# A feed-forward stage emitted as one chain of slots, with weight factors made three slots ahead

## The chip, the core and the metric

The kernel runs on one core of a Trainium2 chip. The metric is device time in microseconds (us) for one launch of the whole program, as the median over runs; lower is better.

## What is computed

The reference is one step of a hybrid decoder layer with 1024 prompt tokens and 8 sample tokens, model width 1024. A feed-forward stage with half weight stands before and after the mixers:

```python
def swiglu(x, w_gate, w_up, w_down):
    return (jax.nn.silu(x @ w_gate) * (x @ w_up)) @ w_down
...
D_FF = ((8 * D_MODEL // 3 + 127) // 128) * 128
...
    x = x + (0.5 * swiglu(rms_norm(x, g_ffn1), w1_gate, w1_up, w1_down)).astype(x.dtype)
...
    x = x + (mixed @ w_out).astype(x.dtype)
    x = x + memory_attend(rms_norm(x, g_cross), mem_k, mem_v, w_cq, w_co).astype(x.dtype)
    x = x + (0.5 * swiglu(rms_norm(x, g_ffn2), w2_gate, w2_up, w2_down)).astype(x.dtype)
```

`D_FF` is 2816, which is 22 blocks of 128 hidden columns. Between the two feed-forward stages lie the attention, state-space and cross-attention stages; the change doesn't touch them. All data is float32.

## The kernel before

The function `ffn` is called twice, here FFN1 and FFN2. Activations lie with the model width on the partitions and the tokens along the row, in three groups: P0 and P1 of 388 tokens and a rest R of 256. A float32 product is made of three matmuls on a high and a low part of each operand (`three`, L332: high by high, high by low, low by high), so every weight tile and every activation is split: ScalarE casts the high part, then VectorE or GpSimd subtracts it for the low part (`split`, L319 and L320, for weights; `put`, L264 and L265, for activations).

P0 and P1 together are computed by a Strassen-Winograd scheme: a two-by-two block product takes seven products in place of eight. The names are those of the scheme: A11, A12, A21, A22 are blocks of weights, S1 to S4 sums of them (`add_up`, L366, on VectorE); B11, B21, B22 and T1 to T4 are the matching activations. The rest R is computed directly from A11, A12, A21 and A22.

`gate_up(m)` makes one block of 128 hidden columns. Its eight weight factors are used in the order of the table `ORDER`. Each product leaves its result in one of three PSUM banks, from which `evac` takes it at once: L399 is the ScalarE copy of bank 1 into bank 2 that seeds it, L402 and L408 copy partial results, L405 and L415 are the silu, L411, L414, L416 and L428 are VectorE work, and L393 (ScalarE `tv`) with L394 (VectorE) forms the rest's hidden values, whose high part is `hRh`.

After two blocks, `down(m)` multiplies the pair of hidden blocks with two rows of the down weights, in two column halves, c = 0 and 1, each for two units (u = 0 and 1). There are two sets of PSUM banks; a unit takes one set and each `gate_up` takes one. L499 seeds bank 2 from bank 1 on ScalarE; L501 to L518 are VectorE's adds from a bank onto the residual `x` in SBUF. A set can be used again only when such an add or copy has read it. The eleventh pair is "plain": it goes through `down_last`, which the change leaves alone (the `pd` products). So there are 20 full pairs in the program, each 396 matmuls at L332: 84 with 388 columns and 48 with 256 in each of its three blocks.

Weights come from HBM by DMAs that SyncE issues, 512 KB each, into two raw buffers (tag `wr`); split factors lie in four buffers (tag `w`):

```python
    def raw_(src):
        t = wp.tile([128, 1040], F32, name="fraw", tag="wr", bufs=2)[:, :1024]
        st["load"] = nc.sync.dma_start(t if len(src.shape) == 2 else t.rearrange("p (k c) -> p k c", c=src.shape[2]), src).ins
        return t
```

The load into a raw buffer is issued when the last engine that reads its old content is done. What sets the order of work on each engine before is the framework's scheduler, which simulates a timeline over the whole program and reorders the source; each engine then takes its instructions strictly in that order, and waits where one isn't ready.

Of the kernel before, what the change touches and what calls it, by code (L numbers as in the profile page):

```python
# [10 lines left out]
F32 = mybir.dt.float32  # L11
# [65 lines left out]
def tile_step(ctx, tc, a, o):  # L77
# [257 lines left out]
    ORDER = (("A11", 0, "B11", True), ("S2", 1, "T2", False), ("A12", 0, "B21", False), ("S3", 1, "T3", False),  # L335
             ("S1", 2, "T1", True), ("S4", 2, "B22", False), ("A22", 1, "T4", False), ("A21", None, None, False))
# [4 lines left out]
    def ffn(x, F, wg, wu, wd, fin, turn, mid=None):  # L341
# [27 lines left out]
        def gate_up(m):  # L369
            q = m % 2  # L370
            g_, u_ = raw_(cols_of(wg, m * 128)), raw_(cols_of(wu, m * 128))
            t = {"A11": g_[:, :512], "A12": g_[:, 512:], "A21": u_[:, :512], "A22": u_[:, 512:]}
            bk, rb = bank_set()
            b1, b2, b3 = bk
            sums = sums_of(m)
            e = {}

            def mat(name):
                if name == "S2":
                    add_up("S1", t, sums[:, :512])  # L380
                if name in SUMS and name not in t:
                    add_up(name, t, sums[:, :512] if name == "S3" else sums[:, 512:1024])
                return split(two(512), t[name])

            def rest(name, w):
                i = name in ("A21", "A22")
                first, last = name in ("A11", "A22"), name in ("A12", "A21")
                for j in range(4):
                    three(rb[:, int(i)], w, j, F["R"][j + (4 if name in ("A12", "A22") else 0)], first and j == 0, last and j == 3)

            def rest_end():
                gr, hr = u1_(NR), u1_(NR)
                nc.scalar.activation(gr, rb[:, 0], AF.Silu)  # L393
                nc.vector.scalar_tensor_tensor(hr, rb[:, 1], 0.5, gr, op0=OP.mult, op1=OP.mult)  # L394
                put(Hd["R"][q], hr, nc.vector)

            def evac(name):
                if name == "A11":
                    nc.scalar.copy(b2, b1)  # L399
                elif name == "S2":  # L400
                    e["U2"] = acc_(PA)
                    nc.scalar.copy(e["U2"], b2)  # L402
                elif name == "A12":
                    e["g0"] = g1_(PA)
                    nc.scalar.activation(e["g0"], b1, AF.Silu)  # L405
                elif name == "S3":
                    e["U3"] = acc_(PA)
                    nc.scalar.copy(e["U3"], b2)  # L408
                elif name == "S1":
                    e["u1"] = sq_(PA)  # L410
                    nc.vector.tensor_add(e["u1"], b3, e["U3"])  # L411
                elif name == "S4":
                    g1, u1 = g1_(PA), e["u1"]
                    nc.vector.tensor_add(g1, b3, e["U2"])  # L414
                    nc.scalar.activation(g1, g1, AF.Silu)  # L415
                    nc.vector.scalar_tensor_tensor(u1, u1, 0.5, g1, op0=OP.mult, op1=OP.mult)  # L416
                    if Hd["plain"]:
                        put(Hd["B22" if q else "B12"], u1, nc.vector)
                    elif q:
                        b12, t1 = Hd["b"]  # L420
                        nc.vector.tensor_sub(t1, u1, t1)
                        put(Hd["T2"], t1, nc.vector)
                        put(Hd["B22"], u1, nc.gpsimd)
                        nc.vector.tensor_sub(b12, u1, b12)
                        put(Hd["T3"], b12, nc.gpsimd)
                elif name == "A22":
                    u0, u1 = sq_(PA), e["u1"]
                    nc.vector.scalar_tensor_tensor(u0, b2, 0.5, e["g0"], op0=OP.mult, op1=OP.mult)  # L428
                    put(Hd["B21" if q else "B11"], u0, nc.vector)
                    if Hd["plain"]:  # L430
                        pass
                    elif q:
                        t2 = Hd["b"][1]
                        nc.vector.tensor_sub(u0, u0, t2)
                        put(Hd["T4"], u0, nc.gpsimd)
                    else:
                        nc.vector.tensor_sub(u0, u1, u0)
                        put(Hd["T1"], u0, nc.gpsimd)
                        Hd["b"] = (u1, u0)

            late = m == 0
            early = {}
            for name, b, f, first in ORDER:
                if late and name == "A21":
                    continue
                if name == "S3":
                    early["S1"] = mat("S1")
                w = early.pop(name, None) or mat(name)
                if f:
                    for j in range(4):  # L450
# [1330 lines left out]
```

## Time and profile before

| what | value |
|---|---|
| median of 3 runs | 2690.99 us (2689.28 to 2700.45) |
| profiled execution, its own time | 2690.33 us |
| its span in the profile | 2688.5 us |
| mean granted TensorE clock | 0.971 of full |
| TensorE busy | 2513.5 us, 93% |
| VectorE, ScalarE, GpSimd busy | 67%, 44%, 34% |
| FFN1, first to last matmul at L332 | 105.7 to 800.7 us |
| FFN2, first to last matmul at L332 | 1949.0 to 2640.4 us |

The span is what the profiler saw between the first and last instruction; the program's own time has 1.8 us more around it. The granted clock is the share of full speed that the chip let TensorE run at.

### The profile page before, as it was taken

How to read it: one execution, taken by the hardware profiler on the slowest of the kernel's cores; microseconds unless marked ns; L12 is line 12 of the kernel's file. 1: busy time of each engine (PE TensorE's matmuls, PEld its weight loads, DVE VectorE, ACT ScalarE, POOL GpSimd, SP SyncE). 2: the span in 40 equal slices, each digit the busy share in tenths (PEclk: the TensorE clock that was granted, in tenths of full speed). 3: DMA queues.
4: the chain of work that ended last, by engine and by line, in shares of the span. 5: the costliest groups of instructions: out<-in, count | busy, mean ns of one | idle time of the engine just before them, and what ended most of it. 6: DMA issues, size and time to landing. Idle time of an engine off the chain costs nothing. (4 is left out here: it accounts for less than half of the span.)

```text
span 2688.5 us, 42038 instructions
## 1 busy us (share of the span) xinstructions
PE 2513.5 (93%) x15999; PEld 2387.5 (89%) x15999; DVE 1809.4 (67%) x3660; ACT 1170.4 (44%) x2415; POOL 907.7 (34%) x675
## 2 busy tenths in 40 slices
PE   6899999999999999988996899989699999999998
PEld 6899999999998999987585899978689999999997
DVE  7566666666656657879578947564776666666665
ACT  5433333333334446554576523232344333333345
POOL 5433333333334111125265644102443333333333
PEclk9999999999999999999997999999899999999999
DMA  5412111211113222335756314573011111111112
GB/s 170 135 49 63 58 56 57 64 57 56 57 50 110 76 63 69 102 116 188 250 168 200 116 54 135 180 228 103 24 40 55 48 48 48 55 48 49 55 48 79
DMA packets 270930, 243.66 MB, mean 91 GB/s; under 512 B 16624, under 2 KB 241064, under 8 KB 270720
## 3 DMA queue, kind: packets, MB, share of 16 engines
q1 hardware_dynamic: 269056, 240.88, 29.1%
q8 instruction: 126, 2.06, 0.3%
q14 instruction: 76, 0.62, 0.1%
q10 hardware_dynamic: 1672, 0.09, 0.0%
HBM read 200.02 MB, written 45.75 MB: 91 GB/s over the span
## 5 line engine op out<-in xcount | busy, mean ns | idle before, releaser
L235 POOL TENSOR_TENSOR wl<-wr,wh 128x1024 fp32r<-128x1024 f32 (+4 forms) x79 | 168.2, 2130 | 562.7 <-ACT wh L231 495.7
L320 POOL TENSOR_TENSOR fw<-fraw,fw 128x512 fp32r<-128x512 f32 x131 | 174.6, 1333 | 469.1 <-ACT fw L319 407.9
L320 POOL TENSOR_TENSOR fw<-fs,fw 128x512 fp32r<-128x512 f32 x128 | 172.5, 1348 | 398.4 <-ACT fw L319 367.2
L319 ACT CAST fw<-fs 128x512 fp32r<-128x512 f32 x256 | 158.3, 618 | 270.1 <-PE fb L332 160.0
L319 ACT CAST fw<-fraw 128x512 fp32r<-128x512 f32 x262 | 162.1, 619 | 192.3 <-PE fb L332 189.0
L366 DVE TENSOR_TENSOR fs<-fraw 128x512 f32<-128x512 f32 (+1 forms) x168 | 100.4, 598 | 138.7 <-DMA fraw<-in_w_up_dram 65.9
L320 DVE TENSOR_TENSOR fw<-fraw,fw 128x512 fp32r<-128x512 f32 x131 | 103.3, 788 | 112.8 <-ACT fw L319 112.7
L320 DVE TENSOR_TENSOR fw<-fs,fw 128x512 fp32r<-128x512 f32 x128 | 95.5, 746 | 97.7 <-ACT fw L319 97.7
L332 PE MATMUL fb<-hRh,fw 128*128 128x256 f32 x640 | 137.3, 280 | 0.5
L231 ACT CAST wh<-wr 128x1024 fp32r<-128x1024 f32 (+1 forms) x80 | 76.7, 959 | 111.5 <-PE pwa L245 43.5
L332 PEld LDWEIGHTS fb<-hRh,fw 128*128 128x128 f32 x640 | 109.2, 188 | 3.7 <-DVE x L516 3.7
L245 PE MATMUL pxbc<-xh,wh 128*128 128x344 f32 x288 | 94.7, 329 | 1.6 <-DVE xr L882 1.6
L245 PE MATMUL pqkv<-xh,wh 128*128 128x344 f32 x288 | 93.9, 326 | 0.4 <-DVE x L546 0.3
L245 PE MATMUL pxbc<-xh,wl 128*128 128x344 f32 x288 | 93.8, 326 | 0.0
L245 PE MATMUL pxbc<-xl,wh 128*128 128x344 f32 x288 | 93.2, 324 | 0.0
L245 PE MATMUL pqkv<-xh,wl 128*128 128x344 f32 x288 | 93.0, 323 | 0.0
L245 PE MATMUL pqkv<-xl,wh 128*128 128x344 f32 x288 | 92.8, 322 | 0.0
L332 PE MATMUL fb<-hRl,fw 128*128 128x256 f32 x320 | 87.7, 278 | 0.0
L411 DVE TENSOR_TENSOR tu<-fb,ts 128x388 f32<-128x388 f32 x44 | 24.7, 562 | 90.3 <-ACT ts L408 90.3
L1052 ACT ACTIVATE pr<-pr,nm 128x128 f32<-128x128 f32 (+3 forms) x64 | 49.9, 779 | 56.9 <-DVE nm L1050 51.7
L1050 DVE CUSTOM_DVE_ANT_0 pr<-ps,U 128x128 f32<-128x128 f32 (+3 forms) x64 | 48.0, 751 | 33.5 <-PE ptr L1065 19.5
L332 PE MATMUL fb<-T2h,fw 128*128 128x388 f32 x160 | 54.6, 362 | 17.0 <-ACT fb L499 17.0
(798 smaller groups left out, 9425.1 us busy)
## 6 DMA issues: line engine op xcount, KB each, us to landing
fraw<-in_w_gate_dram SPq DMA_DIRECT2D x44, 512.0 KB
fraw<-in_w_up_dram SPq DMA_DIRECT2D x44, 512.0 KB
fraw<-in_w_down_dram SPq DMA_DIRECT2D x44, 512.0 KB
wr<-in_w_in_dram SPq DMA_DIRECT2D x32, 512.0 KB
x_scr<-x SPq DMA_DIRECT2D x16, 516.0 KB
x<-x_scr SPq DMA_DIRECT2D x16, 516.0 KB
bc<-acs_scr SPq DMA_DIRECT2D x16, 512.0 KB
ckv<-in_cache_mem_k_dram SPq DMA_DIRECT2D x16, 512.0 KB
```

Of the source, the lines that this page charges most:

```text
L231: nc.scalar.copy(hi[:, :w], raw[:, :w])
L235: e.tensor_sub(lo[:, q], raw[:, q], hi[:, q].bitcast(F32))
L245: nc.tensor.matmul(ps, w, v, start=i == 0, stop=i == last)
L319: nc.scalar.copy(hi, src)
L320: (nc.vector if st["turn"] else nc.gpsimd).tensor_sub(lo, src, hi.bitcast(F32))
L332: nc.tensor.matmul(ps, l[:, js], m, start=bool(start and not i), stop=bool(stop and i == 2), skip_group_check=True)
L366: nc.vector.tensor_tensor(dst, t[p], t[q], op=op)
L411: nc.vector.tensor_add(e["u1"], b3, e["U3"])
L1050: nc.vector.tensor_tensor_reduce(pr[:, :w], ps[:, :w], U[:, 896 - b * 128:1024], -1.0, 3e38, OP.add, OP.min, nm)
L1052: nc.scalar.activation(pr[:, :w], pr[:, :w], AF.Exp, scale=-1.0, bias=nm, accum_out=sm)
```

## The change

`gate_up` and `down` no longer emit instructions. They return lists of slots; a slot is a maker of weight factors, the product that uses them, and evacuation events. A new function `run` strings the slots of all pairs into one chain. For slot i it emits first the weight factors of slot i+3 (the load, the sums, the cast, the subtraction), then the matmuls of slot i, then one pending event of each earlier slot, then the first event of slot i. On TensorE, VectorE, ScalarE and GpSimd the order of execution within `ffn` is that of this emission; SyncE's queue is still ordered by the scheduler.

Besides that: S1 is now the second product of `gate_up` and comes before S2; its result is copied aside on ScalarE, and S3's result is added from its bank in place of being copied. In `down` the four weight factors of a half are used in the order A11 with A21 (`first`), S1 with S2 (`sums12`), S3 with S4 (`sums34`), A12 with A22 (`final`). The low parts of all `down` factors go to GpSimd (before, VectorE and GpSimd took turns). The add of a `down` unit onto P0 after A12 becomes `moved`: a ScalarE copy out of the bank and a GpSimd add, in place of one VectorE add (80 of each in the program). The matmuls are the same in number and size. VectorE has 160 instruction rows fewer, GpSimd 160 more.

```diff
-    def split(hl, src, like=lambda t: t):
+    def split(hl, src, like=lambda t: t, eng=None):
         hi, lo = like(hl[0]), like(hl[1])
-        st["turn"] = not st.get("turn")
+        if not eng:
+            st["turn"] = not st.get("turn")
+            eng = nc.vector if st["turn"] else nc.gpsimd
         nc.scalar.copy(hi, src)
-        (nc.vector if st["turn"] else nc.gpsimd).tensor_sub(lo, src, hi.bitcast(F32))
+        eng.tensor_sub(lo, src, hi.bitcast(F32))
...
+            for name, b, f, first, evs in (
+                    ("A11", 0, "B11", True, (seed,)), ("S1", 2, "T1", True, (kept("s1", 2),)), ("S2", 1, "T2", False, (kept("U2", 1),)),
+                    ("A12", 0, "B21", False, (silu,)), ("S3", 1, "T3", False, (up1,)), ("S4", 2, "B22", False, (gate1, hid1, hid1b)),
+                    ("A22", 1, "T4", False, (hid0, hid0b)), ("A21", None, None, False, (rest_end, rest_end2))):
...
+                out.append((lambda name=name: mat(name), product(name, b, f, first, late), evs))
...
+                    if names[0] in SUMS:
+                        i = 0 if names[0] == "S1" else 2
+                        for j, nm in enumerate(names):
+                            add_up(nm, t, t["sums"][:, (i + j) * 256:(i + j + 1) * 256])
+                        hl = split(two(512), t["sums"][:, i * 256:(i + 2) * 256], eng=nc.gpsimd)
...
+                        hl = split(two(512), t["wa" if names[0] == "A11" else "wb"], twice, eng=nc.gpsimd)
...
+                def add(x_, b):
+                    nc.vector.tensor_add(x_, x_, b)
+                def moved(x_, b):
+                    t_ = acc_(PA)
+                    nc.scalar.copy(t_, b)
+                    nc.gpsimd.tensor_add(x_, x_, t_)
+                def first(W, c=c, U=U):
+                    for u in range(2):
+                        bk, r2 = bank_set()
+                        U.append({"b": bk, "x": (x[2 * c + u], x[2 * c + u + 4]), "r": r2, "j": u})
+                    for e in U:
+                        three(e["b"][0], W[0], e["j"], Hd["B11"], True, True)
+                        nc.scalar.copy(e["b"][1], e["b"][0])
+                    for i in range(2):
                         for e in U:
+                            three(e["r"][:, i], W[i], e["j"], Hd["R"][0], i == 0, False)
+                def sums12(W, U=U):
+                    for i, b, f, r_ in ((0, 2, "T1", 1), (1, 1, "T2", 0)):
                         for e in U:
+                            three(e["b"][b], W[i], e["j"], Hd[f], i == 0, True)
+                            add(e["x"][r_][:, P1], e["b"][b])
+                def sums34(W, U=U):
+                    for i, b, f, r_ in ((1, 2, "B22", 0), (0, 1, "T3", 1)):
+                        for e in U:
+                            three(e["b"][b], W[i], e["j"], Hd[f], False, True)
+                            add(e["x"][r_][:, P1], e["b"][b])
+                def final(W, U=U):
+                    for i, b, f in ((0, 0, "B21"), (1, 1, "T4")):
+                        for e in U:
+                            three(e["b"][b], W[i], e["j"], Hd[f], False, True)
+                            if i:
+                                add(e["x"][1][:, P0], e["b"][1])
+                            else:
+                                moved(e["x"][0][:, P0], e["b"][0])
+                        for e in U:
+                            three(e["r"][:, i], W[i], e["j"], Hd["R"][1], False, True)
+                            add(e["x"][i][:, R], e["r"][:, i])
+                for names, mm in ((("A11", "A21"), first), (("S1", "S2"), sums12), (("S3", "S4"), sums34), (("A12", "A22"), final)):
+                    out.append((lambda names=names, mats=mats: mats(names), mm, ()))
+            return out
...
+        AHEAD = 3
+        def run(units):
+            slots, W, left = [], {}, []
+            for before, unit, after in units:
+                u = unit()
+                for i, sl in enumerate(u):
+                    slots.append(sl + (before if not i else None, after if i + 1 == len(u) else None))
+            for i in range(-AHEAD, len(slots)):
+                if i + AHEAD < len(slots):
+                    W[i + AHEAD] = slots[i + AHEAD][0]()
+                if i < 0:
+                    continue
+                _, mm, evs, before, after = slots[i]
+                if before:
+                    before()
+                mm(W.pop(i))
+                todo, left = left, []
+                for evs_ in todo + [evs]:
+                    if evs_:
+                        evs_[0]()
+                        left.append(evs_[1:])
+                if after:
+                    after()
...
+        with tc.manual_schedule(engines={E_.PE, E_.DVE, E_.Activation, E_.Pool}):
+            run(units)
```

In the changed kernel the cast and subtraction of `split` are L321 and L322, `add_up` is L364, the rest's silu and product L400 and L401, `put` still L264 and L265, the seeds of `down` L514, its VectorE adds L500, and `moved` is L505 (ScalarE) and L506 (GpSimd). `fb` are PSUM banks, `fs` a tile of weight sums, `fw` a split weight factor, `fraw` a raw weight buffer, `tu`, `tg`, `ts` and `tv` temporaries of hidden values, `x0` to `x7` the residual.

On ScalarE, from the last silu of a pair's second `gate_up` to the first seeds of its `down`, the kernel before has:

```order
L393 ACTIVATE tv_2908<-fb_1268 128x256
L319 CAST fw_2943<-fs_1497 128x512
L264 CAST hRh_2523<-tv_2909 128x256
L319 CAST fw_2962<-fraw_2916 128x512
L415 ACTIVATE tg_2847<-tg_2847 128x388
L319 CAST fw_2983<-fs_1497 128x512
L499 COPY fb_1270<-fb_1269 128x388
L499 COPY fb_1266<-fb_1265 128x388
L264 CAST T2h_2513<-tu_2675 128x388
```

and the changed kernel:

```order
L426 ACTIVATE tg_2258<-tg_2258 128x388
L321 CAST fw_2263<-fs_1457 128x512
L264 CAST T2h_1930<-tu_2100 128x388
L264 CAST B21h_1926<-tu_2294 128x388
L321 CAST fw_2300<-fs_1457 128x512
L264 CAST B22h_1928<-tu_2237 128x388
L264 CAST T3h_1932<-tu_2047 128x388
L264 CAST T4h_1936<-tu_2294 128x388
L400 ACTIVATE tv_2323<-fb_1268 128x256
L321 CAST fw_2328<-fraw_2241 128x512
L514 COPY fb_1270<-fb_1269 128x388
L514 COPY fb_1266<-fb_1265 128x388
```

The rest's silu (`tv`, which reads the bank that `down`'s unit 1 writes next) stood ahead of the pair's last gate silu and of every T and B cast; now it stands behind two weight casts and all five casts of hidden values.

On VectorE, at the end of a `down` (its half c = 1, whose residual rows are `x2`, `x3`, `x6`, `x7`), where the sums for the next `gate_up` are formed from its freshly loaded up weights, the kernel before has:

```order
L505 TENSOR_TENSOR x5_165<-x5_165,fb_1266 128x388
L507 TENSOR_TENSOR x6_166<-x6_166,fb_1271 128x388
L507 TENSOR_TENSOR x7_167<-x7_167,fb_1267 128x388
L516 TENSOR_TENSOR x2_162<-x2_162,fb_1272 128x256
L516 TENSOR_TENSOR x3_163<-x3_163,fb_1268 128x256
L320 TENSOR_TENSOR fw_1861<-fs_1497,fw_1861 128x512
L366 TENSOR_TENSOR fs_1497<-fraw_1916 128x512
L511 TENSOR_TENSOR x4_164<-x4_164,fb_1270 128x388
L511 TENSOR_TENSOR x5_165<-x5_165,fb_1266 128x388
```

and the changed kernel:

```order
L500 TENSOR_TENSOR x2_162<-x2_162,fb_1270 128x388
L500 TENSOR_TENSOR x3_163<-x3_163,fb_1266 128x388
L364 TENSOR_TENSOR fs_1457<-fraw_2459 128x512
L322 TENSOR_TENSOR fw_2481<-fs_1457,fw_2481 128x512
L500 TENSOR_TENSOR x2_162<-x2_162,fb_1271 128x388
L500 TENSOR_TENSOR x3_163<-x3_163,fb_1267 128x388
L500 TENSOR_TENSOR x6_166<-x6_166,fb_1270 128x388
L500 TENSOR_TENSOR x7_167<-x7_167,fb_1266 128x388
```

The sum over the new load (`fraw_2459`, a tile of `in_w_up`) stood ahead of two P1 adds; now the sum and the subtraction that splits it stand ahead of four.

On GpSimd at the same place (the second half's factors) the changed kernel has:

```order
L322 TENSOR_TENSOR fw_2374<-fs_1457,fw_2374 128x512
L322 TENSOR_TENSOR fw_2395<-fs_1457,fw_2395 128x512
L506 TENSOR_TENSOR x0_160<-x0_160,ts_2401 128x388
L506 TENSOR_TENSOR x1_161<-x1_161,ts_2407 128x388
L322 TENSOR_TENSOR fw_2434<-fraw_2241,fw_2434 128x512
L322 TENSOR_TENSOR fw_2461<-fraw_2457,fw_2461 128x512
```

where the kernel before has, between the casts of hidden values and the next pair:

```order
L265 TENSOR_TENSOR T3l_1284<-tu_1383,T3h_1283 128x388
L320 TENSOR_TENSOR fw_1840<-fraw_1694,fw_1840 128x512
L265 TENSOR_TENSOR T4l_1288<-tu_1652,T4h_1287 128x388
L320 TENSOR_TENSOR fw_1918<-fraw_1914,fw_1918 128x512
```

The subtraction that reads the second down row's raw tile for the last time (`fraw_2241` in the changed kernel) stands now behind two subtractions and two `moved` adds on GpSimd. The next up weights are loaded into that buffer.

## Rows read from the trace of the kernel before

**Rows 1.** Windows: busy time of each engine, granted clock, DMA share, GB/s.

```profile
197.15:217.85 20.70, 20.70 (x134) 20.70 (x133) 10.16 (x21) 8.61 (x17) 6.30 (x6) 1.00 0.16 51
2044.71:2065.31 20.60, 20.60 (x133) 20.60 (x133) 10.66 (x19) 8.73 (x19) 7.54 (x6) 1.00 0.16 52
1985.00:2600.00 615.00, 608.41 (x3810) 591.25 (x3810) 406.27 (x769) 239.63 (x470) 199.83 (x155) 1.00 0.17 50
```

**Rows 2.** Timeline of TensorE, one matmul nine pairs apart: start us, us, what.

```profile
175.59 0.34 PE L332 MATMUL fb<-T3h,fw 128*128 128x388 f32 x1
758.59 0.34 PE L332 MATMUL fb<-T3h,fw 128*128 128x388 f32 x1
2023.25 0.34 PE L332 MATMUL fb<-T3h,fw 128*128 128x388 f32 x1
2598.44 0.34 PE L332 MATMUL fb<-T3h,fw 128*128 128x388 f32 x1
```

**Rows 3.** Chain of waits of TensorE in FFN1, then FFN2: us, times, longest.

```profile
PE fb L332 <- ACT fb L499: 17.0, 10, 2.7
PE fb L332 <- DVE x L507: 5.3, 10, 0.5
```

**Rows 4.** Timeline, end of a down in FFN1.

```profile
688.77 0.69 DVE L366 TENSOR_TENSOR fs<-fraw 128x512 f32<-128x512 f32 x1 [2.55 <-DMA fraw<-in_w_up_dram]
689.38 1.02 DVE L511 TENSOR_TENSOR x<-x,fb 128x388 f32<-128x388 f32 x2
689.97 0.94 ACT L499 COPY fb<-fb 128x388 f32<-128x388 f32 x2 [3.30 <-DVE x L511]
690.49 0.69 PE L332 MATMUL fb<-T2h,fw 128*128 128x388 f32 x1 [2.71 <-ACT fb L499]
```

**Rows 5.** Windows: right behind that wait, and after.

```profile
690.49:693.90 3.41, 3.41 (x13) 3.41 (x14) 2.76 (x6) 0.41 (x1) 0.00 (x0) 0.51 0.00 0
694.00:697.40 3.40, 3.40 (x23) 3.40 (x22) 2.09 (x5) 0.62 (x1) 0.00 (x0) 1.00 0.00 0
```

**Rows 6.** Timeline, a weight load in FFN2: release, issue, use.

```profile
2525.93 0.69 DVE L320 TENSOR_TENSOR fw<-fraw,fw 128x512 fp32r<-128x512 f32 x1
2526.65 0.38 SPq L325 DMA_DIRECT2D fraw<-in_w_up_dram  x1
2530.67 0.70 DVE L366 TENSOR_TENSOR fs<-fraw 128x512 f32<-128x512 f32 x1 [0.28 <-DMA fraw<-in_w_up_dram]
```

**Rows 7.** Groups by line and form, FFN2: count | busy us, mean ns | idle before.

```profile
L319 ACT CAST fw<-fraw 128x512 fp32r<-128x512 f32 x84 | 52.1, 620 | 56.2 <-PE fb L332 56.2
L366 DVE TENSOR_TENSOR fs<-fraw 128x256 f32<-128x256 f32 x28 | 11.8, 422 | 34.3 <-POOL fw L320 23.8 <-DMA fraw<-in_w_down_dram 10.5
L503 DVE TENSOR_TENSOR x<-x,fb 128x388 f32<-128x388 f32 x29 | 16.0, 553 | 0.0
L393 ACT ACTIVATE tv<-fb 128x256 f32<-128x256 f32 x14 | 5.4, 383 | 26.1 <-PE fb L332 26.1
L265 DVE TENSOR_TENSOR T2l<-tu,T2h 128x388 fp32r<-128x388 f32 x7 | 6.3, 907 | 0.0
L264 ACT CAST T2h<-tu 128x388 fp32r<-128x388 f32 x7 | 3.6, 518 | 2.7 <-DVE tu L421 2.7
```

**Rows 8.** Timeline, VectorE and GpSimd at once.

```profile
2513.46 1.29 POOL L320 TENSOR_TENSOR fw<-fs,fw 128x512 fp32r<-128x512 f32 x1 [1.23 <-ACT fw L319]
2513.68 1.35 DVE L366 TENSOR_TENSOR fs<-fs,fraw 128x256 f32<-128x256 f32 x1
```

**Rows 9.** Timeline of TensorE: FFN1's start, its end (pd), FFN2's start.

```profile
110.66 0.69 PE L332 MATMUL fb<-T20h,fw 128*128 128x388 f32 x1 [2.73 <-ACT fb L399]
801.87 0.45 PE L245 MATMUL pd<-B11h,lwh 128*128 128x388 f32 x1 [0.83 <-ACT lwh L264]
806.52 1.34 PE L245 MATMUL pd<-B21l,lwh 128*128 128x388 f32 x3 [1.45 <-DVE B21l L265]
1956.68 0.66 PE L332 MATMUL fb<-T20h,fw 128*128 128x388 f32 x1 [3.49 <-ACT fb L399]
```

More of the change, by code (lines that the diff above doesn't have):

```diff
@@ L370, in gate_up @@
             q = m % 2
[L371 to L376, printed above, removed]
+            t, e, out = {}, {}, []
             def mat(name):
-                if name == "S2":
-                    add_up("S1", t, sums[:, :512])
+                if not t:
+                    g_, u_ = raw_(cols_of(wg, m * 128)), raw_(cols_of(wu, m * 128))
+                    t.update(A11=g_[:, :512], A12=g_[:, 512:], A21=u_[:, :512], A22=u_[:, 512:], sums=sums_of(m))
                 if name in SUMS and name not in t:
-                    add_up(name, t, sums[:, :512] if name == "S3" else sums[:, 512:1024])
+                    sums = t["sums"]
+                    add_up(name, t, sums[:, :512] if name in ("S1", "S3") else sums[:, 512:1024])
                 return split(two(512), t[name])
@@ new lines, in rest, with product, mm @@
+                    three(e["rb"][:, int(i)], w, j, F["R"][j + (4 if name in ("A12", "A22") else 0)], first and j == 0, last and j == 3)
+            def product(name, b, f, first, late):
+                def mm(w):
+                    if not e:
+                        e["bk"], e["rb"] = bank_set()
+                    if f:
+                        for j in range(4):
+                            three(e["bk"][b], w, j, F[f][j], first and j == 0, j == 3)
+                    if name[0] == "A" and not late:
+                        rest(name, w)
+                return mm
@@ L444, in gate_up @@
                 if late and name == "A21":
                     continue
[L446 to L450, printed above, removed]
-                        three(bk[b], w, j, F[f][j], first and j == 0, j == 3)
-                if f:
-                    evac(name)
-                if name[0] == "A" and not late:
-                    rest(name, w)
+                out.append((lambda name=name: mat(name), product(name, b, f, first, late), evs))
@@ L464, in down @@
             twice = lambda t: t.rearrange("p (i c) -> p i c", i=2)
             for c in range(2):
-                cs = slice(c * 256, (c + 1) * 256)
-                wa, wb = twice(ra)[:, :, cs], twice(rb_)[:, :, cs]
-                t = {"A11": wa[:, 0], "A21": wa[:, 1], "A12": wb[:, 0], "A22": wb[:, 1]}
-                W = {}
-                def pair(names, src):
-                    hi, lo = split(two(512), src, twice if len(src.shape) == 3 else (lambda x: x))
-                    for i, name in enumerate(names):
-                        W[name] = hi[:, i * 256:(i + 1) * 256], lo[:, i * 256:(i + 1) * 256]
@@ L476, in need @@
-                def need(name):
-                    if name in W:
-                        return
-                    if name in ("A11", "A21"):
-                        pair(("A11", "A21"), wa)
-                    elif name in ("A12", "A22"):
-                        pair(("A12", "A22"), wb)
-                    else:
-                        i = 0 if name in ("S1", "S2") else 2
-                        for j, nm in enumerate((("S1", "S2"), ("S3", "S4"))[i // 2]):
-                            add_up(nm, t, sums[:, (i + j) * 256:(i + j + 1) * 256])
-                        pair(("S1", "S2") if i == 0 else ("S3", "S4"), sums[:, i * 256:(i + 2) * 256])
@@ L549, in ffn, with hidden @@
         last = DFF // 128 - 2
-        for m in range(0, DFF // 128, 2):
+        def hidden(m):
             for nm in MATS if m < last else ("B11", "B12", "B21", "B22"):
```

182 lines of the change are left out of this document (79 added, 103 removed).

## The prediction

> **What bounds the kernel now.** I read the windows first, for a stretch that the change can't improve and for the steady state. In the steady part of FFN2 TensorE works 608.41 of 615 us, VectorE 406.27, ScalarE 239.63, GpSimd 199.83 [rows 1]. TensorE is the bound, so only what it waits for can be won. The same rows give its price without waits: a block of 132 matmuls inside `gate_up` takes 20.60 us in FFN2 and 20.70 in FFN1. With 84 x 388 + 48 x 256 = 44,880 columns in 20.60 us, a column costs 0.459 ns, a 388-column matmul 0.178 us and a 256-column one 0.118. A pair of three such blocks would take 61.8 us (FFN2) or 62.1 (FFN1).
>
> Then the timeline, for what a pair takes: the same matmul nine pairs apart starts at 175.59 and 758.59, so 64.78 us per pair in FFN1, and at 2023.25 and 2598.44, 63.91 in FFN2 [rows 2]. A pair loses 2.7 and 2.1 us. With ten pairs each, **48 us** in all can be won in steady state.
>
> The waits say where: in `down`. In FFN1 TensorE waits ten times for the seed L499, 17.0 us; in FFN2 it waits in small pieces for adds like L507, 5.3 us [rows 3]; the rest is what follows a wait. One wait of FFN1 taken apart [rows 4]: VectorE sits 2.55 us in `add_up` until the up weights land (688.77); the adds L511 that stand behind it run at 689.38; the seed at 689.97 waits for these; the matmul starts at 690.49, 2.71 us late. The wait is not work that is missing but work that is ready and stands behind a DMA. After it TensorE is at 0.51 of full speed (the lower of its two levels, 1.2 GHz) for 3.41 us: 13 matmuls where 23 go in as much time at full clock [rows 5]. Ten matmuls of about 0.15 us are 1.5 us more.
>
> The edges of the stages lose too [rows 9]: 2.73 us at FFN1's start and 3.49 at FFN2's, both for the seed that T2's product needs, and 0.83 and 1.45 us at FFN1's end.
>
> **What the change removes.** If every `down` wait went, 48 us. At the starts S1 with T1 comes second, and T2 and its weights have 2 us longer: I take back 3.5 + 1.5 us (a clock drop) at FFN2's start and 1.5 of 2.73 at FFN1's, where weights are late as well. At the ends A22 and A21 now follow S4, so the last hidden values get ready under products: 3 us of the waits and the low clock behind them, twice. Together **12 us**; bounds 0 (other late factors take their place) and 18. 160 fewer VectorE rows, and 80 adds that become a copy and a GpSimd add, cost nothing by themselves, since those engines idle a third of the time or more; without that cover it is a ScalarE copy of about 0.47 (half of the pair of 0.94 in [rows 4]) a time, 38 us in all.
>
> **What it adds: first wait, at the start of a down.** I lay out a pair with time 0 at the second `gate_up`'s A11. By the matmul prices the slots start at: S1 3.54, S2 5.66, A12 7.79, S3 11.33, S4 13.45, A22 15.57, A21 19.11, `first` 20.53. In `first`, unit 1's rest product goes into the bank that the second `gate_up`'s rest still holds; it is wanted at 20.53 + 1.07 + 0.35 = 21.95. It must wait for VectorE L401, which waits for `tv` on ScalarE, which now stands behind two casts of sums and all T and B casts.
>
> When is `tv` done? The second down row goes into the raw buffer that A21's subtraction frees: slot S3 starts at 11.33, a buffer is free 0.2 later, cast 0.62, subtraction 0.69 as in the rows of the other loads [rows 6, 7]: 12.9. From release to use such a load takes 4.0 us (2526.62 to 2530.67) [rows 6], so 16.9. VectorE meanwhile stands in `add_up` for `sums12` and does nothing else. From there, by [rows 7]: two sums 0.42 each, two passes over 388 columns 0.55 each (taken as the add's 0.553), the T2h cast 0.52, T2l 0.91, B21's product 0.55, its cast 0.52 and subtraction 0.55, the sums for `sums34` 0.42 and some 0.6 (one beside GpSimd), the cast of these 0.62, then B22h, T3h and T4h 3 x 0.52, `tv` 0.38 and the product L401 0.42 (as a 256-column sum). That is 9.1 us; five changes of engine add 0.05 each, and some ten instructions that follow on one engine start 0.08 before the one ahead ends (689.38 against 688.77 + 0.69 in [rows 4]). 16.9 + 9.1 + 0.25 - 0.8 gives 25.4; because ScalarE takes B22h ahead of the last sums' cast when it can, I take 25.2. The wait is **3.2 us**. Without blocked VectorE instructions 0.5 less, with more overlap of the hand-offs 2.0; with two more sums blocked 3.9.
>
> How VectorE blocks is in [rows 8]: a 256-column sum that takes 0.42 alone took 1.35 beside a GpSimd subtraction of 1.29 that had begun 0.22 earlier; and T2l takes 0.91 where other passes over 388 columns take 0.55 [rows 7]. The Trainium skill ("SBUF — State Buffer", "🎯 Summary: rules for kernel authors") says that VectorE with two SBUF inputs and a GpSimd instruction that reads SBUF exclude each other, the second one being blocked until the first is done; the trace agrees, with those 1.35 us. It speaks against a change that moves subtractions and adds onto GpSimd.
>
> **Second wait, at the end of a down.** T4's product of unit 0 in the second half's `final` goes into the bank that T3's product of `sums34` filled, so it needs the VectorE add to `x6`. That add stands behind the next pair's S1 sum over the up weights, a subtraction, and two adds. The up weights go into the raw buffer that GpSimd's subtraction for `final` frees, which stands behind a subtraction and two `moved` adds. Counted from the end of the first half's `sums34`: 0.2 until its last bank is read, add 0.55, two sums 0.8, cast 0.65, GpSimd subtraction 1.3, two `moved` adds 1.95 (1.29 x 388/512 each), subtraction 1.27, load 4.05, sum 0.69, cast 0.65, subtraction 0.69, three adds 1.4: 14.2. TensorE gets there after `final` 3.54, `first` 2.48, `sums12` and `sums34` 2.13 each and 1.77 of `final`: 12.05. So 2.15 late, and **3.1** if the sum and subtractions of this chain are blocked about as in [rows 8] (0.95 together). Bounds: 1.2 if the GpSimd queue ahead costs nothing, 3.6 with one more block. SyncE's later loads queue behind this one, and wait as long.
>
> This is the wait of [rows 4] again, with more adds behind the same sum.
>
> **Smaller ones.** In the first half's `final` T4 waits for the T3 add, late by VectorE's backlog, or `first` for the L505 copy behind a cast: 0.8 (0 to 1.1). A11 or the second rest product behind S2's sum at the end: 0.3 (0 to 0.5). Per pair 3.2 + 3.1 + 0.8 + 0.3 = 7.4. Both large waits are longer than the 2.71 after which the clock fell; I count one fall of 1.5 us a pair (0 to two): **8.9 us**, times 20 pairs 178.
>
> The sum is made on the profiled execution, 2690.33 us, which is the median, 2690.99, but for 0.7: 2690 - 48 - 12 + 178 = 2808.
>
> **The rivals.** *Both chains are in time*: all waits go, 2690 - 60 = 2630. For it: in FFN2 the same kind of load costs VectorE 0.28 us only [rows 6]. Against it: there VectorE's own subtraction freed the buffer, here GpSimd's behind four others. It decides in favour where new waits and clock falls stay under 60/20 = 3.0 us a pair.
>
> *Only one of the two waits is real*, the other being hidden by it since a late TensorE gives the other engines time: 3.1 + 1.1 + 0.75 of clock = 4.95 a pair, 2690 - 60 + 99 = 2729. For it: in [rows 4] one stop lets everything catch up. Against: the two lie 17 us apart, each with its own load.
>
> *GpSimd blocks VectorE nearly every time*: 3.9 + 1.1 + 3.6 + 0.5 + 3.0 of clock = 12.1 a pair, 2690 - 60 + 242 = 2872. This is what the skill's rule on the shared port ("SBUF — State Buffer") would make of it if instructions always met; [rows 8] show that they do when they meet, not how often.
>
> *The change does no more than swap waits*: three slots ahead needs raw tiles, of which there are two, so the new waits come to about the 3.0 a pair that are won: 2690, within 0.5%.
>
> **How the numbers follow.** Chances: the forecast 0.55, blocked nearly always 0.10, one wait 0.17, a swap 0.07, both in time 0.11. The lower bounds of all waits (2.0 + 1.2, no falls) give 64 - 60, about 2694, so the range begins at 2690; it ends at 2865, near the third rival. Outside lie the faster case and the ends of two others. About 0.5% (13 us) is what a measurement here can tell from no change: faster 0.11, same 0.07, slower 0.82. I predict 2808.
>
> **What would show it.** The waits of TensorE in the changed profile should name VectorE's L401 or its add L500 twice a pair, about 3 us each, and VectorE should idle before `add_up` L364 for the loads of `in_w_down` and `in_w_up`. Pairs should lie about 70 us apart, with stretches at the lower clock behind the waits. At FFN2's start the wait of 3.49 should be gone. I am wrong if the loads are issued sooner than the subtractions say, or if `tv` is not waited for by `first`.

## The result and the profile after

The changed kernel takes 2827.31 us (median of 4 runs, 2822.18 to 2828.68) against 2692.22 (4 runs on the same chips): 1.0495 times the kernel before, 95% interval 1.0476 to 1.0513. It is slower by 135 us; 2808, 118 more than before, had been forecast. The profiled execution took 2822.18 us with a span of 2820.0.

TensorE's waits in FFN1 (first two rows) and FFN2 answer to [rows 3]; columns are us, times, longest:

```profile
PE fb L334 <- DVE tv L401: 33.3, 10, 3.8
PE fb L334 <- DVE x L500: 30.7, 14, 3.1
...
PE fb L334 <- DVE tv L401: 35.8, 10, 3.9
PE fb L334 <- DVE x L500: 29.2, 31, 1.7
```

Both waits of the forecast are there. The one for the rest's product comes once in each of the twenty pairs, 3.1 to 3.9 us long. The one for the adds comes once in each pair of FFN1, 2.8 to 3.1 us long; in FFN2 it is three shorter waits, together 2.8 to 3.0 us. The old waits for the seeds of `down` are gone. The same matmul eight pairs apart, as in [rows 2]:

```profile
179.67 0.53 PE L334 MATMUL fb<-B110h,fw 128*128 128x388 f32 x1
753.40 0.53 PE L334 MATMUL fb<-B110h,fw 128*128 128x388 f32 x1
...
2087.94 0.53 PE L334 MATMUL fb<-B110h,fw 128*128 128x388 f32 x1
2662.00 0.33 PE L334 MATMUL fb<-B110h,fw 128*128 128x388 f32 x1
```

(753.40 - 179.67)/8 = 71.7 us a pair in FFN1, 71.8 in FFN2; before it was 64.8 and 63.9. That is 6.9 and 7.9 more, times ten each 148 us. The windows over these stretches give the granted clock in the column before the last two, 0.95 (before, 1.00 over most of FFN2 in [rows 1]), and the third row is the window behind one of the waits, the counterpart of [rows 5]:

```profile
2087.94:2662.00 574.06, 522.30 (x3169) 513.96 (x3169) 313.42 (x568) 213.61 (x424) 230.68 (x193) 0.95 0.15 45
179.67:753.40 573.73, 522.35 (x3170) 516.93 (x3169) 308.68 (x569) 212.96 (x424) 234.06 (x193) 0.95 0.17 52
2564.90:2568.30 3.40, 3.39 (x14) 3.39 (x15) 0.52 (x2) 1.72 (x5) 3.40 (x4) 0.50 0.00 0
```

How the first wait comes about, in the timeline of one pair of FFN2 (start us, us, what; in brackets the idle time before and its releaser):

```profile
2551.56 1.29 POOL L322 TENSOR_TENSOR fw<-fraw,fw 128x512 fp32r<-128x512 f32 x1 [1.77 <-ACT fw L321]
2552.88 0.34 SPq L327 DMA_DIRECT2D fraw<-in_w_down_dram  x1
...
2556.25 0.42 DVE L364 TENSOR_TENSOR fs<-fraw 128x256 f32<-128x256 f32 x1 [0.64 <-DMA fraw<-in_w_down_dram]
...
2558.86 0.99 DVE L265 TENSOR_TENSOR T2l<-tu,T2h 128x388 fp32r<-128x388 f32 x1 [0.58 <-ACT T2h L264]
...
2563.61 0.51 ACT L264 CAST T4h<-tu 128x388 fp32r<-128x388 f32 x1
2564.02 0.37 ACT L400 ACTIVATE tv<-fb 128x256 f32<-128x256 f32 x1
2564.43 0.42 DVE L401 SCALAR_TENSOR_TENSOR tv<-fb,tv 128x256 f32<-128x256 f32 x1 [1.34 <-ACT tv L400]
2564.91 0.58 PE L334 MATMUL fb<-hRh,fw 128*128 128x256 f32 x1 [3.54 <-DVE tv L401]
```

GpSimd's subtraction frees the raw buffer and the second down row is loaded into it. VectorE waits for it to land, goes to and fro with ScalarE over the casts, and `tv`, which needs nothing of all that, starts when the cast of T4 is through. The second wait, in FFN1, is [rows 4] again with another victim (there the adds behind the sum, L511, go onto P0, not P1):

```profile
664.05 1.95 DVE L500 TENSOR_TENSOR x<-x,fb 128x388 f32<-128x388 f32 x4
665.92 0.59 DVE L364 TENSOR_TENSOR fs<-fraw 128x256 f32<-128x256 f32 x1
...
668.91 2.00 POOL L506 TENSOR_TENSOR x<-x,ts 128x388 f32<-128x388 f32 x2
670.86 2.55 POOL L322 TENSOR_TENSOR fw<-fraw,fw 128x512 fp32r<-128x512 f32 x2
672.19 0.38 SPq L327 DMA_DIRECT2D fraw<-in_w_up_dram  x1
676.28 0.69 DVE L364 TENSOR_TENSOR fs<-fraw 128x512 f32<-128x512 f32 x1 [2.66 <-DMA fraw<-in_w_up_dram]
677.71 0.69 DVE L322 TENSOR_TENSOR fw<-fs,fw 128x512 fp32r<-128x512 f32 x1 [0.74 <-ACT fw L321]
678.32 1.96 DVE L500 TENSOR_TENSOR x<-x,fb 128x388 f32<-128x388 f32 x4
679.87 0.69 PE L334 MATMUL fb<-T4h,fw 128*128 128x388 f32 x1 [2.93 <-DVE x L500]
```

GpSimd's subtraction frees the raw tile behind the two `moved` adds, the load goes out 0.04 us after the first of the two subtractions ends (670.86 + 1.29), its sum runs 4.1 us later, and four adds that were ready stand behind sum and subtraction.

### The profile page after: what moved, and what is told of

It is laid out like the page before. It is cut to its first block, busy times and chain, and to the rows that moved or that the text cites. A ratio compares the mean times of both kernels' runs of the same rounds, so it can differ in the third digit from the quotient of the medians.

```text
span 2820.0 us, 42185 instructions
## 1 busy us (share of the span) xinstructions
PE 2550.0 (90%) x15999; PEld 2429.3 (86%) x15999; DVE 1752.1 (62%) x3500; ACT 1205.0 (43%) x2495; POOL 1082.5 (38%) x835
## 4 chain that ended last, share of the span: by engine, by line
PE 28%; DVE 14%; DMA 6%; issue 5%; ACT 4%; POOL 3%; SPq 0%; DVEq 0%; ACTq 0%; POOLq 0%
PE fb L334 13%; PE pcq L245 2%; PE pxbc L245 2%; PE pco L245 2%; POOL fw L322 2%; DVE x L500 2%; DMA bc<-acs_scr 2%; DVE fs L364 1%; DMA fraw<-in_w_down_dram 1%; PE pwa L245 1%; PE pwo L245 1%; PE pwb L245 1%; DMA fraw<-in_w_up_dram 1%; ACT fw L321 1%; PE pzz L245 1%
## 5 line engine op out<-in xcount | busy, mean ns | idle before, releaser
L322 POOL TENSOR_TENSOR fw<-fs,fw 128x512 fp32r<-128x512 f32 x168 | 220.0, 1310 | 633.5 <-ACT fw L321 633.5
L321 ACT CAST fw<-fs 128x512 fp32r<-128x512 f32 x256 | 158.8, 620 | 480.6 <-DVE fs L364 410.2
L322 POOL TENSOR_TENSOR fw<-fraw,fw 128x512 fp32r<-128x512 f32 x171 | 220.8, 1298 | 210.9 <-ACT fw L321 210.9
L500 DVE TENSOR_TENSOR x<-x,fb 128x388 f32<-128x388 f32 (+1 forms) x560 | 259.4, 512 | 67.8 <-PE fb L334 66.1
L334 PE MATMUL fb<-hRh,fw 128*128 128x256 f32 x640 | 156.4, 312 | 87.1 <-DVE tv L401 69.1
L321 ACT CAST fw<-fraw 128x512 fp32r<-128x512 f32 x262 | 161.9, 618 | 169.8 <-PE fb L334 153.8
L334 PEld LDWEIGHTS fb<-hRh,fw 128*128 128x128 f32 x640 | 122.0, 214 | 97.4 <-DVE tv L401 73.1
L322 DVE TENSOR_TENSOR fw<-fraw,fw 128x512 fp32r<-128x512 f32 x91 | 77.4, 850 | 178.8 <-ACT fw L321 173.3
L364 DVE TENSOR_TENSOR fs<-fraw 128x512 f32<-128x512 f32 (+1 forms) x168 | 116.3, 692 | 82.2 <-DMA fraw<-in_w_up_dram 69.8
L322 DVE TENSOR_TENSOR fw<-fs,fw 128x512 fp32r<-128x512 f32 x88 | 65.5, 745 | 108.9 <-ACT fw L321 108.9
L334 PE MATMUL fb<-hRl,fw 128*128 128x256 f32 x320 | 97.2, 304 | 0.0
L334 PE MATMUL fb<-T4h,fw 128*128 128x388 f32 x160 | 55.6, 390 | 38.8 <-DVE x L500 38.8
L506 POOL TENSOR_TENSOR x<-x,ts 128x388 f32<-128x388 f32 x80 | 83.1, 1062 | 17.1 <-ACT ts L505 17.1
```

Source lines behind the costliest of these rows:

```text
L322: eng.tensor_sub(lo, src, hi.bitcast(F32))
L364: nc.vector.tensor_tensor(dst, t[p], t[q], op=op)
L500: nc.vector.tensor_add(x_, x_, b)
L506: nc.gpsimd.tensor_add(x_, x_, t_)
```

## The experiments

All start from the changed kernel unless another is named. The theory: the order in which VectorE and ScalarE take their work makes the waits, because sums over a load that hasn't landed stand ahead of evacuations that are ready. The first rival: the work moved to GpSimd makes them, by blocking VectorE or by freeing raw tiles late. The second: the loads are late in themselves, whatever stands behind them. Times of "before" are those of the same chip; between the chips they differ by up to 10 us (2683 to 2693), so a difference from the changed kernel's 2827.31 is good to about that. The first three experiments and the two with two slots ahead are one run each.

**GpSimd's new work undone.**

```diff
-                        hl = split(two(512), t["sums"][:, i * 256:(i + 2) * 256], eng=nc.gpsimd)
+                        hl = split(two(512), t["sums"][:, i * 256:(i + 2) * 256])
...
-                                moved(e["x"][0][:, P0], e["b"][0])
+                                add(e["x"][0][:, P0], e["b"][0])
```

> The changed kernel, but the low parts of the down factors are made in turn by VectorE and GpSimd again, and the add after A12 is a VectorE add again (no copy, no GpSimd add). If the order is the cause (weights and sums emitted ahead of the evacuations): the wait at the start of a down for the rest's product L401 stays at 2.8 us or more, the one at the end of a down falls to about 1 since GpSimd's queue ahead of the raw buffer's release is shorter, and the time is 2740 to 2780 us. If the work moved to GpSimd is the cause: both waits fall under 1 us and the time is under 2710.

2865.42 us (before 2693.44): slower still by 38 us, which neither theory had said. The four rows of waits for L401 and L500 add up to 172 us in place of 129. Those in FFN2:

```profile
PE fb L334 <- DVE tv L401: 52.4, 10, 5.4
PE fb L334 <- DVE x L500: 45.2, 21, 2.6
```

In this order work taken from GpSimd goes into the queue that everything stands in. In one pair the factor's subtraction L322 itself stands on VectorE between the sums and L401 (2291.81, after 0.76 idle for its cast), and L442 behind it took 1.36 us in place of 0.56. So GpSimd's share isn't what makes the source's order slow. Which of the two undone moves costs more was not separated.

**The rest's evacuation first.**

```diff
+                rest_first = bool(evs) and evs[0].__name__ == "rest_end"
+                if rest_first:
+                    slots[i][1](W.pop(i))
+                    evs[0]()
+                    evs = evs[1:]
                 if i + AHEAD < len(slots):
                     W[i + AHEAD] = slots[i + AHEAD][0]()
...
-                mm(W.pop(i))
+                if not rest_first:
+                    mm(W.pop(i))
```

> The changed kernel, but in the slot of A21 the rest's silu and product (tv, L401) are emitted ahead of the slot's weight factors and of the pending events. If the order is the cause and the two waits of a pair are independent: the wait of TensorE for L401 falls from 3.4 to under 0.6 us in all twenty pairs, the waits for the adds to x stay at 3 to 4 us a pair, and the time is 2730 to 2760. If a late TensorE at the start of a down only gave the other engines time: what is won there comes back as a longer wait at the end of the down, and the time is 2790 or more.

2786.66 us (before 2693.44), 41 less than the changed kernel, where 70 to 95 were expected (2730 to 2760). FFN2's waits:

```profile
PE fb L334 <- DVE x L500: 36.6, 40, 1.7
PE fb L334 <- ACT fb L514: 14.8, 10, 1.7
PE fb L334 <- DVE tv L401: 5.1, 10, 0.7
```

The wait for L401 fell from 35.8 to 5.1, as the theory has it; 14.8 came back as a wait for the seeds L514, which stand behind the same casts, and 7.4 as adds.

**The adds of down first.**

```diff
+                adds = i >= 0 and slots[i][1].__name__ in ("first", "sums12", "sums34", "final")
+                if adds:
+                    slots[i][1](W.pop(i))
                 if i + AHEAD < len(slots):
                     W[i + AHEAD] = slots[i + AHEAD][0]()
...
-                mm(W.pop(i))
+                if not adds:
+                    mm(W.pop(i))
```

> The changed kernel, but in the slots of down the products and the adds to x are emitted ahead of the factors of three slots later. If the order is the cause and the waits are independent: the waits for the adds to x fall under 1 us a pair, the wait for L401 stays at 3.3 to 4 us, and the time is 2740 to 2770. If the late load itself is the cause (the sum over it is needed, whatever stands behind it): TensorE waits for the factor of S1 in place of the add, about as long, and the time stays over 2800.

2792.47 us (before 2693.44), where 2740 to 2770 was expected. The wait for adds fell from 29.2 to 13.3 us in FFN2 but only from 30.7 to 26.2 in FFN1, that for L401 stayed (35.8). The late-load rival's sign, TensorE waiting for S1's factor, isn't in the waits. What failed in the expectation is that one slot is not enough: the load's sum now stood behind the adds of `sums34` and ahead of those of `final`.

**Both.** Edit: the two above together.

> Both changes of order together, the rest's evacuation and the adds of down ahead of the factors; GpSimd's work as in the changed kernel. If the order is the cause of both waits: a pair takes 62 to 63.5 us, and the time is 2630 to 2670, below the kernel before. If GpSimd's share or the late loads bound the pair: new waits of 2 us or more a pair, 2700 or more.

2737.13 us (before 2693.44): ratio 1.0166 (1.0143 to 1.0188). Together the edits give 90 us, more than the 41 and 35 that they give alone, but the waits for seeds (16.2 us in FFN2) and adds (13.0) are left. My 2630 to 2670 was a miss.

**Two slots ahead.** `AHEAD = 2`, alone and with both edits.

> The changed kernel with its factors two slots ahead in place of three, and nothing else. If VectorE's stand in front of loads that haven't landed is the cause: sums are emitted a slot later, when the load is nearer, so less is queued behind the wait; the waits for L401 and the adds fall from 7.3 to about 3 to 5 us a pair and the time is 2720 to 2780. If the lead of the factors is what the pair lives on: TensorE waits for factors (L321, L322) instead, and the time is 2830 or more.

> Two slots ahead, and the rest's evacuation and the adds of down ahead of the factors. If only the order of loads' sums against evacuations counts: under 2690. If a factor made behind the adds and only two slots ahead comes late: a new wait of about 2 us for the second half's S1 with S2 (sums, cast and GpSimd subtraction take 2.8 us and more after adds that end 1.4 us into a slot of 2.48), and 2700 to 2750.

Alone 2796.64 us, with both edits 2831.19 (before 2683.07). Alone, the waits for adds fell to 12.6 in FFN2 and 24.3 in FFN1, while L401 kept 34.1 and 34.0: the smaller lead helps at the end of a `down`, in part. With the adds ahead as well, the factors themselves came late:

```profile
PE fb L334 <- ACT fw L321: 24.3, 20, 2.3
PE fb L334 <- POOL fw L322: 23.2, 33, 1.3
```

**Sums behind the adds only where a load is waited for.**

```diff
+                if name == "S1" and m and not q:
+                    mm.__name__ = "hold"
+                if q and name == "A22":
+                    mm.__name__ = "late"
+                if name == "A21":
+                    mm.__name__ = "rest"
...
+                    if c and names[0] in ("S3", "A12"):
+                        mm.__name__ = "late"
...
+                if name in ("late", "rest"):
+                    slots[i][1](W.pop(i))
...
+                for j in (i + 2, i + AHEAD):
+                    if 0 <= j < len(slots) and j not in made and not (j == i + AHEAD and slots[j][1].__name__ == "hold"):
+                        W[j] = slots[j][0]()
+                        made.add(j)
...
```

A slot named `late` or `rest` emits its products and evacuations ahead of the factors; `hold` has S1's factor made two slots ahead.

> Three slots ahead as in the changed kernel, except where a load is waited for: the evacuations come ahead of the factors in the slots A22 and A21 of a pair's second gate_up and in the second half's last two slots of down, and the sum S1 of the next gate_up is made two slots ahead, behind the adds. If VectorE standing in front of a load with evacuations behind it is the whole cause: the waits for L401 and the adds fall to under 1.5 us a pair, a pair takes 62.5 to 64 us, and the time is 2630 to 2670, under the kernel before. If the late load itself is the cause: TensorE waits for the factor S1 at the next gate_up, 2 us or more, and the time is 2700 or more.

2736.18 us, ratio 1.0194 (1.0170 to 1.0218): not under the kernel before, where 2630 to 2670 was expected. But the end of a `down` is clear, with the same load, GpSimd share and slots: adds (L506 here) cost 6.0 us in FFN2 in place of 29.2, and no factor of these pairs is waited for instead. There the late load is not a wait of TensorE's once nothing stands behind it. At the start were left the seeds (L520 here) and the rest's product (L407 here):

```profile
PE fb L334 <- ACT fb L520: 20.2, 10, 2.0
PE fb L334 <- DVE tv L407: 11.3, 10, 1.1
PE fb L334 <- DVE x L506: 6.0, 18, 0.6
```

**The scheduler's order.** The changed kernel with the context that fixes the order taken away.

```diff
-        with tc.manual_schedule(engines={E_.PE, E_.DVE, E_.Activation, E_.Pool}):
+        with nullcontext():
```

> The changed kernel, the same slots, products and shares of the engines, but the order on TensorE, VectorE, ScalarE and GpSimd is the scheduler's again. If the order as in the source is the cause: the waits for L401 and the adds fall under 3 us a pair, a pair takes 62.5 to 64.5 us and the time is 2640 to 2710. If the slots themselves (the products' order, the work moved to GpSimd) cost the time: 2760 or more.

2727.83 us, ratio 1.0161 (1.0131 to 1.0191): about 100 us of the 135 go with the order alone, though 2640 to 2710 was expected. The adds' wait is gone; L401's is not (31.1 us in FFN1, 30.6 in FFN2). One pair:

```profile
412.56 3.21 POOL L322 TENSOR_TENSOR fw<-fs,fw 128x512 fp32r<-128x512 f32 x2 [2.79 <-ACT fw L321]
412.95 1.66 DVE L442 TENSOR_TENSOR tu<-tu 128x388 f32<-128x388 f32 x1
415.95 0.38 ACT L400 ACTIVATE tv<-fb 128x256 f32<-128x256 f32 x1
416.12 1.29 POOL L265 TENSOR_TENSOR B22l<-tu,B22h 128x388 fp32r<-128x388 f32 x1 [0.36 <-ACT B22h L264]
416.45 1.38 DVE L265 TENSOR_TENSOR B21l<-tu,B21h 128x388 fp32r<-128x388 f32 x1
417.37 1.58 POOL L322 TENSOR_TENSOR fw<-fraw,fw 128x512 fp32r<-128x512 f32 x1
417.75 1.48 DVE L364 TENSOR_TENSOR fs<-fs,fraw 128x256 f32<-128x256 f32 x1
418.91 1.18 POOL L265 TENSOR_TENSOR T3l<-tu,T3h 128x388 fp32r<-128x388 f32 x1
419.16 1.36 DVE L455 TENSOR_TENSOR tu<-tu 128x388 f32<-128x388 f32 x1
420.90 0.39 PE L334 MATMUL fb<-hRh,fw 128*128 128x256 f32 x1 [3.23 <-DVE tv L401]
```

`tv` had been ready since 416.33 (415.95 + 0.38 on ScalarE). VectorE was the late one: instructions that take 0.42 to 0.56 alone took 1.4 to 1.7 each while GpSimd worked beside them.

**The scheduler's order and GpSimd undone.** Edits of the first experiment and the one above.

> As e8_scheduler_order, with GpSimd's new work undone as well (down's low parts in turn on VectorE and GpSimd, the add after A12 on VectorE). If the wait for L401 that e8 keeps (3.1 us a pair) is VectorE blocked by GpSimd (its subtractions took 1.2 to 1.7 us in place of 0.55 there): it falls under 1.5 us, and the time is 2650 to 2695. If it is the late load or the scheduler's place for L401: it stays over 2.5, and the time is 2715 or more.

2693.39 us, ratio 1.0011 (0.9994 to 1.0029): no different from before. L401's wait fell from 31.1 to 6.1 us in FFN1, but only from 30.6 to 19.2 in FFN2, and adds cost 12.1 again in FFN1. So GpSimd's share makes most of L401's wait in FFN1, by blocking as in the rows above; what the rest of FFN2's wait is made of stays open. Here taking GpSimd's share back gains 34 us; under the source's order it cost 38.

**Three more steps of order by hand.** On top of the late sums, first the two sums put into VectorE's gaps between T2's and B21's casts and low parts, with the seeds ahead of the casts that follow and B22's low part on VectorE; then the seeds right behind `tv`, and `hRl` behind the first adds; last the first half's `final` low part on VectorE. Of the edits, one piece of each:

```diff
-                    put(Hd["T2"], t1, nc.vector)
+                    nc.scalar.copy(Hd["T2"][0], t1)
+                    lows.append((Hd["T2"], t1))
...
+                    if name == "restq":
+                        slots[i + 1][1](W.pop(i + 1))
+                        left.pop(0)[0]()
...
+                    elif names[0] == "A12" and not c:
+                        hl = two(512)
+                        nc.scalar.copy(twice(hl[0]), t["wb"])
+                        lows2.append((hl, t["wb"], twice))
...
```

> As e7_late_sums, and at the start of a down: the two sums after the load stand in VectorE's gaps between the casts of T2 and B21 and their subtractions, the seeds of down come ahead of the casts of B22, T3, T4 and hRh, and B22's low part goes to VectorE. If what is left in e7 (1.1 us for L401 and 2.0 for the seeds, a pair) is VectorE going to and fro with ScalarE behind a late load: both fall under 0.5 us, a pair takes 62 to 63.5 us, and the time is 2640 to 2680. If GpSimd is then the bound (three subtractions and two casts' low parts in 5 us): waits for L322 or T3l of 1 us or more, 2700 or more.

> As e9_sums_in_gaps, and the seeds of down come right behind tv on ScalarE, the casts of B22 and T3 behind them, their low parts behind the next factors' sums, and hRl behind the first four adds to x. If what e9 keeps (2.4 to 2.8 us a pair for the add of T1's product) is only the adds' place behind these on VectorE: it falls under 0.8 us, a pair takes 62.5 to 64 us, and the time is 2640 to 2675, under the kernel before. If VectorE or GpSimd has no room left in the first slots of a down: a new wait of 1.5 us or more, 2685 or more.

> As e11_seeds_with_tv, and the low part of the first half's final factor is made by VectorE behind the adds of sums12, in place of GpSimd. If what e11 keeps (1.2 us a pair for that factor from GpSimd, and about 1 for adds behind sums that GpSimd blocks) is GpSimd's queue: both fall under 0.5 us, a pair takes 62.3 to 63.5 us, and the time is 2645 to 2670, clearly below the kernel before. If VectorE's queue is as full: the waits for adds grow as much, and the time stays at 2680 to 2690.

The first: 2708.61 us, ratio 1.0085 (1.0060 to 1.0111), where 2640 to 2680 was expected. The waits for the rest's product and for the seeds are gone, with the same loads; the adds came back with 27.9 us in FFN1 and 33.1 in FFN2. The second: **2684.63**, ratio 0.9984 (0.9969 to 0.9998), 143 us under the changed kernel and level with the kernel before, since 0.2% is less than tells anything here. A pair takes 64.1 us in FFN1 and 64.6 in FFN2, at a granted clock of 1.00. Its expected 2640 to 2675 was missed; FFN1's waits say why:

```profile
PE fb L334 <- POOL fw L322: 9.1, 11, 0.8
PE fb L334 <- DVE x L513: 6.2, 10, 0.6
```

The third: 2689.47, ratio 1.0018 (1.0006 to 1.0030). GpSimd's wait went (0.7 us, once) and the adds' rose to 20.4, as the rival had it: in the first slots of a `down` neither engine had room for that subtraction.

## Why the prediction was right

**What bounds it.** Read rightly: TensorE with its waits. The pairs' own waits of before are gone, so the 48 us of the pairs were there to be won. The edges gave 15.5 us for the 12 forecast, read off the timeline's first and last matmuls of each stage: 0.8 ahead of FFN1 (104.83 for 105.66), 0.8 and 4.35 in the first 132 matmuls of the two stages (24.71 for 25.52, 27.39 for 31.74; the wait of 3.49 in [rows 9] is now 1.49), 6.6 between the stages (1141.7 for 1148.3) and 2.9 behind the last. Of the 6.6, 4.2 lie at FFN1's end, from its last matmul at L332 (now L334) to its last `pd` product (31.95 for 36.14), where 3 were forecast; the other 2.4 lie in the stages that the change doesn't touch, had not been forecast, and their cause stays open.

**First wait.** Forecast 3.2, measured 3.3 (FFN1) and 3.6 (FFN2) on average, with the name, queue and load forecast. The second edit shows that the place of `tv` is its cause. In FFN1 the terms hold too: in the pair whose wait ends at 657.76, slot S3 starts at 643.61, the load goes out at 645.27 and VectorE's sum over it starts at 649.18, 5.6 us into the slot as forecast. In FFN2 the agreement is in part luck: there GpSimd makes the subtraction that frees the buffer (2551.56, 1.29 us for the 0.69 counted), so the load goes out 0.7 us later than forecast, but its sum starts 3.4 us after the release in place of 4.0. The prediction's terms behind the load add up to 9.0, not 9.1, and those ahead of it to 12.84, not 12.9, which moves the wait by less than 0.2. GpSimd's part depends on the order: under the source's order it blocked little here (T2l 0.99, most others 0.56); under the scheduler's order it was most of the same wait in FFN1.

**Second wait.** Forecast 3.1, measured 2.8 to 3.1 in FFN1, as one wait for T4's bank. Its chain is right, but the 0.95 us counted for blocking came out in size and not in kind. In the rows of the pair shown for FFN1 the chain takes 15.2 us in place of 14.2 (from 664.71, where `final`'s first matmul starts, to 679.87): a blocked sum is 0.17 of that (0.59 us for 0.42), 0.46 comes from the sums starting behind a run of four adds (664.05 + 1.95), of which only the last was counted, and the rest from pieces under 0.2 us. The sum and subtraction behind the load took 0.69 each, unblocked.

In FFN2 the forecast of this wait holds only in its total. There GpSimd makes S1's low part (the turns of `split` fall otherwise), so VectorE has one subtraction less ahead of the adds, and T4's bank costs 0.91 us in the pair of these rows, besides 0.27 for B22's:

```profile
2586.49 0.45 PE L334 MATMUL fb<-T4h,fw 128*128 128x388 f32 x1 [0.91 <-DVE x L500]
2586.82 0.82 DVE L364 TENSOR_TENSOR fs<-fs,fraw 128x512 f32<-128x512 f32 x1
2588.38 0.69 DVE L322 TENSOR_TENSOR fw<-fs,fw 128x512 fp32r<-128x512 f32 x1 [0.74 <-ACT fw L321]
2588.99 0.41 DVE L500 TENSOR_TENSOR x<-x,fb 128x256 f32<-128x256 f32 x1
2589.45 0.38 PE L334 MATMUL fb<-hRh,fw 128*128 128x256 f32 x1 [1.64 <-DVE x L500]
```

The largest piece, 1.64 us, is another wait: the second rest product stands behind an add that stands behind S2's sum and subtraction, which the prediction had among its smaller waits at 0.3. That the three come to 29.2 us over ten pairs, as much as FFN1's one wait, is luck.

**Smaller waits.** Forecast 1.1; all waits together are 6.4 and 6.5 us a pair, against 7.4 forecast. In FFN1 this term was too large (four waits of 0.3 in ten pairs); in FFN2 it holds the 1.64.

**The clock.** This term was too small: 1.5 us a pair. A pair takes 71.7 to 71.8, less 61.9 without waits and 6.5 of waits leaves 3.4. The rows with the clock agree: at 0.95 over 574 us, 5% of 574 us over eight pairs is 3.6. The windows behind the two waits of a pair of FFN1 (first two rows) and of FFN2 show where it goes:

```profile
659.30:662.40 3.10, 3.10 (x11) 3.10 (x11) 1.69 (x4) 0.48 (x1) 3.10 (x3) 0.50 0.00 0
679.87:682.90 3.03, 3.03 (x11) 3.03 (x12) 2.75 (x7) 1.39 (x3) 1.23 (x1) 0.50 0.00 0
2564.90:2570.50 5.60, 5.59 (x20) 5.59 (x21) 1.90 (x4) 1.72 (x5) 4.93 (x5) 0.50 0.00 0
2586.50:2590.00 3.50, 1.86 (x10) 1.54 (x11) 2.76 (x6) 1.38 (x3) 1.79 (x3) 1.00 0.02 5
```

In FFN1 the clock is at the lower level (1.2 GHz) behind both waits, two falls where I had counted one. In FFN2 there is one fall, as counted, behind the first wait, but it is about twice as long; the three pieces of the second are followed by none.

**The sum.** Forecast -48 + 178 - 12 = 118; measured 148 - 15.5 by the parts, which is 132, and 131.5 by the two spans. The number is close because errors offset each other: over twenty pairs the waits were put about 19 us too high and the clock about 38 too low. The rival "one wait" fell: neither hid the other. "Both in time" did not happen. Blocking as in "blocked nearly always" shows in the rows of the scheduler's order, and little in those of the changed kernel.

**What stays open.** Whether a third raw tile would have removed both waits wasn't tried. Nor is it shown how far the pair can go: the best order by hand still has 2.2 to 2.7 us a pair above the 61.9.

## What to carry to other kernels

Where each engine takes its work strictly in order, emit whatever waits for a load behind everything whose inputs are ready, above all behind what frees a PSUM bank; "factors as early as possible" does the opposite, and what was to be a lead of three slots brings the wait forward. There is a limit on the other side: with two slots and everything ready first, the factors themselves came late. Moving work to an idle engine is judged with the order it will run in: the same move to GpSimd was worth 38 us in one order and cost 34 in another. And waits of TensorE are priced with the clock behind them: here 6.5 us of waits a pair cost 3.4 more.

## What the hardware showed that was not expected

VectorE's blocking by GpSimd adds up over a run of instructions: in the scheduler's order the four in the rows took 5.9 us where they take about 2.1 alone. The Trainium skill ("SBUF — State Buffer", "Terms") says that the loser of the shared port pair fully blocks; the trace agrees, with 1.38 us for a 388-column subtraction, 0.56 alone, that started 0.33 us into a GpSimd subtraction of 1.29.
